# Second block's recurrent input projection by seven half products, in pairs of heads

## Chip, cores and metric

One NeuronCore of a Trainium2 chip runs the whole kernel. The metric is the device time of one execution in microseconds (us); less is better. The kernel before takes 2208.46 us (median of three runs, 2200.77 to 2210.29).

## What is computed

Two layers over 2048 tokens of width 1024, fp32. Layer 1 is a gated MLP with a spatial mix, layer 2 a gated linear recurrence. The change concerns the input projection of layer 2, `h @ w_in`, here for 12 heads of 128 columns, each with a recurrent column block (x) and a gate column block (g):

```python
xb, g = jnp.split(h @ w_in, 2, axis=-1)             # (2048 x 1024) @ (1024 x 3072)
xc = conv_b + conv_w[3] * xb + ...                  # causal convolution, 4 taps, per channel
r = sigmoid(xh @ gate_a_w + gate_a_b)               # per head, 128 x 128
i = sigmoid(xh @ gate_x_w + gate_x_b)
a = exp(-8 * r * softplus(-lam))
hseq = scan(a, sqrt(1 - a * a) * (i * xc))          # h = a * h + b along the tokens
y = hseq * silu(g);  x = x + y @ w_out
```

## The kernel before

**Blocks and stages.** The 2048 tokens are taken in two blocks of 1024 (`NB`, index `i`). A block goes through layer 1's values (`a_values`), layer 1's gates (`a_gates`), layer 1's output projection (`out_round`, four rounds), layer 2's input projection with its heads (`b_branch`), and layer 2's output projection (`b_out`, and `b_close` in the last block). Channels lie on the 128 partitions, tokens along the free axis. State that crosses from block 0 to block 1 is the convolution's `halo` and the scan's `state`.

**Three passes.** fp32 operands are split into a high and a low part of type fp32r (`split`, L90: a cast on ScalarE, a subtraction on VectorE), and a product is three matmuls (`mm3`, L378: high-high, high-low, low-high). A matmul is 128 x 128 by 128 x 512.

**Half products.** Layer 1 multiplies 2 x 2 blocks with seven products in place of eight (Strassen's method in Winograd's form). The matrix is halved twice: features by columns of the weight, and tokens into two halves of 512. `prep_item` (L187) makes the seven weight operands of an item from two loads of 512 KB with four additions of 128 x 512 and seven splits; `Sums` (L549) makes the seven operands of the activations, each a tile of pool `tops` (14 slots). A `Pair` (L575) is one item: steps `p1` to `p7` of 12 matmuls each (four feature blocks by three passes), which accumulate into a PSUM tile `J` of two halves and a PSUM tile `Y`, with copies on ScalarE and additions on VectorE between them that give two output tiles `oa` and `ob`. A step that adds on into a half of `J` has to wait for the copy that reads that half. `run_pairs` (L625) interleaves the steps of a pair with the last two of the pair before: 1, -4, 5, -3, 6, 2, 7 (minus: of the pair before).

**Layer 2's input projection** is done with all eight blocks. `b_branch` (L998) takes head after head: `proj` (L1004) is 48 matmuls for x (tile `px`) and 48 for g (`pg`); then `Head.conv`, `gates` (12 matmuls into `pr` and `pi`), `decay`, `silu` and `scan` on VectorE and ScalarE, one head behind. The activations `hb` are eight tiles of `tops`; the RMS factor `rbb` multiplies `px` and `pg` as they are read from PSUM (L936, L957). The weights `wb` come from HBM and are split in both blocks (`prep_two`, L238).

**Order.** A list `stream` (L288 to L339) holds every weight tile in the order of use; `take` (L373) makes tiles up to four ahead and loads raw data up to eight ahead. Entries without a key (items made ahead) are made where they stand in the list and written to HBM (`keep`, L221); `load_item` (L228) reads them back in block 1, or later in block 0. In block 0's `a_gates` the eight items of the output projection are made ahead in this way. All transfers are issued on SyncE's queue (SP). Tiles come from pools: `wops` 8 (weight operands), `raws` 4, `work` 12 (tag `wk`: 128 x 1028 fp32; the heads' tiles, `x` and layer 1's `u` and `g`), `pjp` 3 of two PSUM banks, `pbp` 2 of one bank. The tile framework fixes each engine's order ahead of the run from the program's order and the dependencies, and puts an instruction that is ready ahead of one that is not.

Of the kernel before, what the change touches and what calls it, by code (L numbers as in the profile page):

```python
# [57 lines left out]
VP = {0: (1, 2, 6, 5, 7, 3, 4), 2: (1, 5, 6, 3, 7, 2, 4)}  # L58

I_V = N_ITEMS  # L60


@with_exitstack
def trunk(ctx: ExitStack, tc: tile.TileContext, xT, WI, WV, WB, WO, WG, par, wsT, bs, outT):
# [201 lines left out]

        return [((i, "g", b), make, load)]

    def woven(items, more={}):

        out, prev = [], None
        for k, it in enumerate([*items, None]):
            o = {key[2]: (key, f, load) for key, f, load in it} if it else {}
            for p in (1, -4, 5, -3, 6, 2, 7):
# [10 lines left out]
        [(None, f, load) for _, f, load in prep_item(0, m, keep=True, use=False)]  # L285
        for m in range(I_AO, N_ITEMS)
    ]
    stream = []  # L288
    for i in range(NB):
        for k, (c, _) in enumerate(VG[i]):  # L290
            units = prep_v(i, k, c)
            stream += units
        if i > 0:
            for p in VP[0]:
                for u in range(4):
                    make = load_item(i, I_V + u)[MADE.index(p)][1]
                    stream.append(((i, "vs", 0, p, u), make, None))
        stream += prep_vs(i)
        more = {}
        if i == 0:  # L300
            for k in range(0, 16, 2):
                n = ahead.pop(0)
                more |= {(k, 6): n[:3], (k, 2): n[3:6], (k, 7): n[6:]}
        stream += woven([prep_item(i, m) for m in range(I_UG, I_AO)], more)
        for m in range(I_AO, N_ITEMS):
            stream += load_item(i, m)
        for n in range(NH):
            tile_x, tile_g = (
                prep_two([(i, "b", n, z, u) for u in range(2)], f"b{i}_{n}{z}", WB[n, z])
                for z in range(2)  # L310
            )
# [313 lines left out]
    def run_pairs(pairs, hooks):  # L625

        prev = None
        for k, q in enumerate([*pairs, None]):
            steps = []
            if q is not None:  # L630
                steps.append(q.p1)
            if prev is not None:
                steps.append(prev.p4)
            if q is not None:
                steps.append(q.p5)
            if prev is not None:
                steps.append(prev.p3)
            if q is not None:
                steps += [q.p6, q.p2, q.p7]
            for n, f in enumerate(steps):  # L640
                f()
                for g in hooks.get((k, n), ()):
                    g()
            prev = q


# [275 lines left out]
    class Head:  # L922
# [9 lines left out]
        def conv(self, px, rb):  # L932

            n = self.n
            xb = work.tile([P, 1028], F32, tag="wk", name=f"xb{self.id}")
            nc.vector.tensor_tensor(  # L936
                xb[:, 3 : 3 + TB].rearrange("p (a t) -> p a t", a=2), px, rb, ALU.mult
            )
# [59 lines left out]
    def b_branch(i, hb, rb, hooks):  # L998
# [22 lines left out]
        for n in range(NH):  # L1021
# [17 lines left out]
            if n > 0:  # L1039
                heads[n - 1].scan()  # L1040
            after(n, 1)
        return yd, heads[-1]

    def load_yb(i, r, yd):

# [198 lines left out]
    for i in range(NB):  # L1244
# [90 lines left out]
        def ready_b(g, a, th, i=i, x=x, xd=xd, nm=nm, hb=hb):  # L1335
# [11 lines left out]
                nm[th].add(t)  # L1347
            return f

        after = {  # L1350
            (g, p): [ready_b(g, a, th)]
            for g in range(2)
            for p, a, th in ((2, 0, 0), (7, 1, 1), (3, 0, 1), (4, 1, 0))
        }
        for r in range(4):
            tp = sy.o
            if r < 3:
# [22 lines left out]
        yd, tail = b_branch(i, hb, rb, {(0, 0): [finish_b]})  # L1380
        y[0] = load_yb(i, 0, yd)
        x = {}
        last = i == NB - 1
# [2 lines left out]
        def reload(*keys, i=i, x=x, xd=xd):  # L1386
            def f():
                for k in keys:
                    x[k] = wk(f"xr{i}_{k[0]}{k[1]}{k[2]}")
                    nc.sync.dma_start(x[k], xd[k])  # L1390
            return f
# [8 lines left out]
                store(i, th, x, r)  # L1400
            return f

        def end_tail(tail=tail):
            tail.gates()
            tail.decay()
            tail.scan()
# [4 lines left out]
        hooks = {0: [end_tail, reload(*xk[2:])], 1: [get_y(2)]}  # L1411
# [18 lines left out]
def pack(a_w_in, a_w_out, b_w_in, b_gate_a_w, b_gate_x_w, b_w_out):  # L1430
# [13 lines left out]

    u, g = quarters(win[:, :AW]), quarters(win[:, 2 * AW :])
    ug = np.stack([u, g], 1).reshape(16, 2, P, 2, 512)
    items = np.concatenate([ug, outs(wout)], 0)

    wb = b_w_in[0].reshape(2, 4, P, 2, NH, P).transpose(4, 3, 2, 0, 1, 5)

# [54 lines left out]
```

## Time and profile before

| | |
|---|---|
| median of three runs | 2208.46 us |
| the profiled execution | 2206.12 us |
| its span in the trace | 2204.4 us |
| TensorE (PE) busy | 2181.9 us, 99% |
| VectorE (DVE) busy | 1573.5 us, 71% |
| ScalarE (ACT) busy | 1165.7 us, 53% |
| transfers | 371.96 MB, 169 GB/s |

The profiled execution is 2.3 us under the median. A busy share of 99% is an average over stages that have different second engines; the windows by stage say more.

### The profile page before, as it was taken

The page shows a single profiled execution, that of the slowest core. Times are in us where ns is not written, and L with a number is a line of the kernel's source. Part 1 is how long each engine was busy: PE and PEld are TensorE (multiplying, and loading weights), DVE is VectorE, ACT ScalarE, POOL GpSimd, SP SyncE. Part 2 cuts the span into 40 slices and gives each one's busy share as a digit, 9 for nine tenths or more (in the row PEclk, how much of TensorE's full clock was granted, in tenths as well). Part 3 has the DMA queues.
Part 4 walks back from the last instruction along what each step waited for, and adds up shares of the span by engine and source line. Part 5 has one row for each costly group of instructions (what it writes and reads, how often), then busy time and mean ns, then how long its engine had stood idle before and what let it go on. Part 6 is the DMA issues. An engine that isn't in the chain of part 4 may idle for free.

```text
span 2204.4 us, 26352 instructions
## 1 busy us (share of the span) xinstructions
PE 2181.9 (99%) x10016; PEld 1813.8 (82%) x10016; DVE 1573.5 (71%) x2004; ACT 1165.7 (53%) x1598; POOL 63.5 (3%) x83
## 2 busy tenths in 40 slices
PE   9999999999999999999999999999999999999998
PEld 7887878888888888888888888888888888888887
DVE  7967777776878778675776665665678767767735
ACT  7535665663225777774343455455522456777611
POOL 0000000000000001010000000000000001101000
PEclk9999999999999999999999999999999999999998
DMA  6565665669764544236276532232597512222412
GB/s 224 168 211 200 230 218 182 222 233 329 289 226 158 179 178 166 91 105 248 76 246 203 176 130 94 98 112 90 176 336 252 196 62 85 95 89 75 179 43 77
DMA packets 141087, 371.96 MB, mean 169 GB/s; under 512 B 11296, under 2 KB 29856, under 8 KB 140960
## 3 DMA queue, kind: packets, MB, share of 16 engines
q1 hardware_dynamic: 140960, 370.27, 48.4%
q8 instruction: 79, 1.29, 0.2%
q14 instruction: 48, 0.39, 0.1%
HBM read 261.70 MB, written 108.53 MB: 168 GB/s over the span
## 4 chain that ended last, share of the span: by engine, by line
PE 90%; DMA 4%; DVE 3%; ACT 2%; issue 1%; SPq 0%; DVEq 0%; ACTq 0%
PE px L380 18%; PE J L380 17%; PE pg L380 12%; PE po L380 10%; PE X L380 8%; PE Y L380 5%; PE pz L380 4%; PE Z L380 4%; PE pv L380 4%; PE ps L869 2%; DMA vl<-vd 2%; PE pc L380 2%; DMA raw<-in_w 2%; PE pi L380 2%; PE pr L380 2%
## 5 line engine op out<-in xcount | busy, mean ns | idle before, releaser
L380 PE MATMUL J<-ha,w 128*128 128x512 f32 x1728 | 411.0, 391 | 6.3 <-ACT u_0a L604 2.3
L380 PEld LDWEIGHTS J<-ha,w 128*128 128x128 f32 x1728 | 323.2, 188 | 77.0 <-ACT u_0a L604 3.2
L380 PE MATMUL px<-hb,wb 128*128 128x512 f32 x1152 | 266.8, 390 | 0.0
L380 PE MATMUL pg<-hb,wb 128*128 128x512 f32 x1152 | 266.0, 390 | 0.0
L380 PEld LDWEIGHTS pg<-hb,wb 128*128 128x128 f32 x1152 | 216.2, 188 | 45.6
L380 PEld LDWEIGHTS px<-hb,wb 128*128 128x128 f32 x1152 | 215.9, 188 | 44.7
L380 PE MATMUL po<-yb,wo 128*128 128x512 f32 x960 | 219.4, 390 | 0.0
L380 PEld LDWEIGHTS po<-yb,wo 128*128 128x128 f32 x960 | 179.9, 188 | 37.2
L380 PE MATMUL X<-ya,w 128*128 128x512 f32 x768 | 183.3, 390 | 0.0
L380 PEld LDWEIGHTS X<-ya,w 128*128 128x128 f32 x768 | 143.7, 188 | 30.3 <-ACT ya L92 0.4
L93 DVE TENSOR_TENSOR w<-raw,w 128x512 fp32r<-128x512 f32 x160 | 108.6, 687 | 65.5 <-ACT w L92 65.3
L92 ACT CAST ya<-ya 128x1024 fp32r<-128x1024 f32 x56 | 57.5, 1051 | 159.8 <-DVE ya L569 100.3
L380 PE MATMUL J<-b,w 128*128 128x512 f32 x576 | 140.2, 391 | 0.0
L92 ACT CAST w<-raw 128x512 fp32r<-128x512 f32 x160 | 97.5, 619 | 74.8 <-issue 39.7
L380 PEld LDWEIGHTS J<-b,w 128*128 128x128 f32 x576 | 107.1, 188 | 21.6
L670 DVE TENSOR_TENSOR x<-x,X 128x1024 f32<-128x1024 f32 x64 | 77.9, 1218 | 31.8 <-PE X L380 31.8
L380 PE MATMUL Y<-b,w 128*128 128x512 f32 x384 | 93.4, 392 | 1.3 <-DVE sp L873 1.2
L947 DVE SCALAR_TENSOR_TENSOR xc<-xb,pp,xc 128x1024 f32<-128x1024 f32 x72 | 92.3, 1281 | 3.4 <-ACT xc L943 2.6
L380 PE MATMUL Z<-ya,w 128*128 128x512 f32 x384 | 92.6, 389 | 0.0
L380 PEld LDWEIGHTS Y<-b,w 128*128 128x128 f32 x384 | 71.0, 188 | 17.7 <-DVE sp L873 3.0
L92 ACT CAST wb<-rb 128x512 fp32r<-128x512 f32 x96 | 57.8, 615 | 52.2 <-PE px L380 22.1
L380 PEld LDWEIGHTS Z<-ya,w 128*128 128x128 f32 x384 | 72.1, 188 | 15.0
(416 smaller groups left out, 3558.5 us busy)
## 6 DMA issues: line engine op xcount, KB each, us to landing
w<-keep SPq DMA_DIRECT2D x140, 512.0 KB, 3.8
keep<-wc SPq DMA_DIRECT2D x84, 512.0 KB, 3.8
raw<-in_w SPq DMA_DIRECT2D x64, 512.0 KB, 4.2
rb<-in_wb SPq DMA_DIRECT2D x48, 512.0 KB, 3.6
vd<-v SPq DMA_DIRECT2D x32, 512.0 KB, 3.0
vl<-vd SPq DMA_DIRECT2D x32, 512.0 KB, 5.1
ya<-ya SPq DMA_DIRECT2D x16, 1024.0 KB, 6.7
yb<-sg SPq DMA_DIRECT2D x24, 512.0 KB, 2.9
```

The costliest lines, as they stand in the source:

```text
L92: nc.scalar.copy(dst[:, 0], src)
L93: nc.vector.tensor_tensor(dst[:, 1], src, dst[:, 0].bitcast(F32), ALU.subtract)
L380: nc.tensor.matmul(out, lhsT=s, rhs=m, start=first and n == 0, stop=last and n == 2, skip_group_check=True,)
L670: nc.vector.tensor_tensor(t, t, acc[z], ALU.add)
L869: nc.tensor.matmul(pS[:, n * P : (n + 1) * P], lhsT=v[j][th][:, n, cc * P : (cc + 1) * P], rhs=wcv[:, j, :], start=True, stop=True,)
L947: nc.vector.scalar_tensor_tensor(xf, xb[:, k : k + TB], col(C_CW + 4 * n + k), xf, ALU.mult, ALU.add)
```

## The change

Block 1's input projection of layer 2 goes through `Pair`, block 0's stays as it is. The 24 column blocks become 12 items (`bi`): an x item and a g item for each two heads.

- **Weights made ahead.** `early_b` makes the 12 items with `prep_item(keep=True)`: the first in block 0's `b_branch` (after head 9), the next two in block 0's `b_out`, nine in block 1's `a_gates`, spread over 16 pairs. Block 1 reads the 84 operands back (`load_item`) and no longer loads and splits its 24 `wb` tiles.
- **Activations.** In block 1's last `out_round` the step `ready_b` (scale and split into eight tiles `hb`) is replaced by `ready_q` (scaled copies in eight `wk` tiles, on ScalarE) and `make_q` (the seven operands of `Sums` for each of two channel groups, 14 tiles of `tops`), and the squares of the norm come in later calls (`norm_q`). `rbb` moves from `tops` to a `wk` tile.
- **Pairs.** `b_pairs` runs 12 pairs in the order 1, 5, -4, 6, 2, -3, 7. The RMS factor is applied to the finished sums (`scale`, `c21`). `conv` then works on the tile in place. The first gates of a round stand behind `p2` of the next x pair, the second behind `p1` of the next g pair.
- **Tail.** Two heads are left for `b_out` in place of one, and `y[2]` is read back one group later.

```diff
+STEPS = (1, -4, 5, -3, 6, 2, 7)
+STEPS_B = (1, 5, -4, 6, 2, -3, 7)
...
+    def early_b(m):
+        return [
+            (None, f, load) for _, f, load in prep_item(
+                0, I_BI + m, keep=True, use=False, src=lambda m, h: WI[m - 4, h]
+            )
+        ]
...
+        else:
+            for k in range(9):
+                n = early_b(3 + k)
+                k = (1, 3, 5, 6, 8, 10, 11, 13, 15)[k]
+                more |= {(k, 6): n[:3], (k, 2): n[3:6], (k, 7): n[6:]}
...
-        for n in range(NH):
+        if i > 0:
+            stream += woven(
+                [load_item(i, I_BI + m) for m in range(N_BI)],
+                {(2 * b + 2, 2): prep_g(i, b) for b in range(5)} | {(12, -3): prep_g(i, 5)},
+                STEPS_B,
+            )
+        for n in range(NH if i == 0 else 0):
...
+            if n == 9:
+                stream += early_b(0)
         for a, g in AG:
+            if i == 0 and g == 0:
+                stream += early_b(1 + a)
...
+    def b_pairs(i, tp, rb, norm):
...
+        def c21(dst, src):
+            nc.vector.tensor_tensor(dst, src, rb[:, 0], ALU.mult)
+
+        def scale(oa, ob):
+            nc.vector.tensor_tensor(oa, oa, rb, ALU.mult)
+            nc.vector.tensor_tensor(ob[:, 1], ob[:, 1], rb[:, 1], ALU.mult)
+
+        def end_x(b):
+            def f(oa, ob):
+                scale(oa, ob)
+                for h in range(2):
+                    heads[2 * b + h].conv(xb[b][h], None)
+            return f
+
+        def end_g(b):
+            def f(oa, ob):
+                scale(oa, ob)
+                for h, t in enumerate((oa, ob)):
+                    nc.scalar.activation(t, t, AF.Silu)
+                    heads[2 * b + h].sg = t
+            return f
+
+        def first_part(n):
+            def f():
+                heads[n].gates()
+                heads[n].decay()
+            return f
+
+        for b in range(6):
+            pairs.append(Pair(i, I_BI + 2 * b, tp, outs_x(b), c21, end_x(b)))
+            pairs.append(Pair(i, I_BI + 2 * b + 1, tp, outs_g(b), c21, end_g(b)))
+            if b < 5:
+                hooks[2 * b + 2, "p2"] = [first_part(2 * b)]
+                hooks[2 * b + 2, "p7"] = [heads[2 * b].scan]
+                hooks[2 * b + 3, "p1"] = [first_part(2 * b + 1), heads[2 * b + 1].scan]
+        hooks[0, "p2"] = [norm]
+        run_pairs(pairs, hooks, STEPS_B)
+        return yd, heads[-2:]
...
+            after = {
+                (0, 2): [ready_q(0, 0, 0)],
+                (0, 7): [ready_q(0, 1, 1), make_q(0, 1)],
+                (0, 3): [ready_q(0, 0, 1), make_q(0, 5)],
+                (0, 4): [ready_q(0, 1, 0)],
+                (1, 1): [make_q(0, 6), norm_q(0, *every)],
+                (1, 6): [make_q(0, 2)],
+                (1, 2): [make_q(0, 7), ready_q(1, 0, 0)],
+                (1, 7): [ready_q(1, 1, 1), make_q(1, 1)],
+                (1, 3): [ready_q(1, 0, 1), make_q(1, 5)],
+                (1, 4): [
+                    ready_q(1, 1, 0), make_q(1, 6), make_q(1, 2), make_q(0, 4), make_q(1, 7),
+                    make_q(1, 4), make_q(0, 3), make_q(1, 3), norm_q(1, *every),
+                ],
+            }
...
-        rb = tops.tile([P, 2, 2, T], F32, tag="top", name=f"rbb{i}")[:, 0]
+        if i == 0:
+            rb = tops.tile([P, 2, 2, T], F32, tag="top", name=f"rbb{i}")[:, 0]
+        else:
+            rb = wk(f"rbb{i}")
...
+            hooks = {
+                0: [end_tail(tail[0]), reload(*xk[2:4])],
+                1: [end_tail(tail[1]), reload(*xk[4:])], 2: [get_y(2)],
+            }
```

## Rows read from the trace of the kernel before

**Rows 1.** The page: busy time by engine, and the granted clock in 40 slices

```profile
PE 2181.9 (99%) x10016; PEld 1813.8 (82%) x10016; DVE 1573.5 (71%) x2004; ACT 1165.7 (53%) x1598; POOL 63.5 (3%) x83
...
PEclk9999999999999999999999999999999999999998
```

**Rows 2.** Windows by stage; the first line names the columns

```profile
core 0: us, PE busy (x) PEld busy (x) DVE busy (x) ACT busy (x) POOL busy (x), PEclk, DMA share, GB/s
187.10:519.30 332.20, 325.66 (x1551) 270.94 (x1549) 252.93 (x359) 199.71 (x331) 0.00 (x0) 1.00 0.63 217
1271.70:1597.10 325.40, 324.34 (x1553) 271.87 (x1552) 200.69 (x279) 173.83 (x281) 0.00 (x0) 1.00 0.34 113
...
1752.50:2051.00 298.50, 298.50 (x1329) 246.87 (x1328) 213.68 (x215) 206.83 (x230) 29.29 (x33) 1.00 0.26 88
1600.00:1752.50 152.50, 152.50 (x673) 125.92 (x673) 120.33 (x115) 39.40 (x51) 0.19 (x1) 1.00 0.75 267
1714.40:1752.50 38.10, 38.10 (x169) 31.45 (x168) 29.37 (x36) 15.14 (x26) 0.00 (x0) 1.00 0.60 200
972.90:1100.00 127.10, 127.10 (x578) 105.53 (x577) 83.19 (x110) 57.85 (x79) 1.67 (x2) 1.00 0.43 153
2051.00:2140.70 89.70, 89.70 (x397) 74.21 (x397) 41.04 (x41) 34.51 (x41) 1.67 (x2) 1.00 0.31 112
```

**Rows 3.** TensorE's timeline in block 1's projection: start, length, line, names, count

```profile
1928.22 11.04 PE L380 MATMUL px<-hb,wb 128*128 128x512 f32 x48
1939.10 0.40 PE L380 MATMUL pr<-xch,wg 128*128 128x512 f32 x1
```

**Rows 4.** TensorE's waits in block 0's gate stage: total us, times, longest

```profile
PE J L380 <- ACT u_0a L604: 1.8, 1, 1.8
...
PE J L380 <- DVE u_3b L614: 1.3, 1, 1.3
```

**Rows 5.** VectorE's groups, block 1's projection (L1344: whole span): count, busy us, mean ns

```profile
L947 DVE SCALAR_TENSOR_TENSOR xc<-xb,pp,xc 128x1024 f32<-128x1024 f32 x36 | 46.1, 1282 | 2.9 <-ACT xc L943 2.3
L93 DVE TENSOR_TENSOR wb<-rb,wb 128x512 fp32r<-128x512 f32 x38 | 26.0, 687 | 9.7 <-ACT wb L92 9.7
L993 DVE TENSOR_TENSOR_SCAN xc<-a,state,gi 128x1024 f32<-128x1024 f32 x10 | 23.5, 2346 | 0.0
L936 DVE TENSOR_TENSOR xb<-px,rbb 128x1024 f32<-128x1024 f32 x12 | 14.6, 1218 | 0.2 <-ACT rbb L517 0.2
...
L1344 DVE SCALAR_TENSOR_TENSOR hb<-x,pp,hb 128x512 fp32r<-128x512 f32 x32 | 22.9, 748 | 2.2 <-ACT hb L1343 2.1
```

**Rows 6.** ScalarE's groups in block 1's projection

```profile
L92 ACT CAST wb<-rb 128x512 fp32r<-128x512 f32 x38 | 23.2, 616 | 34.2 <-PE px L380 17.2 <-PE pg L380 17.0
L943 ACT ACTIVATE xc<-xb,pp 128x1024 f32<-128x1024 f32 x12 | 15.0, 1252 | 9.7 <-DVE xb L936 9.7
...
L974 ACT ACT_TABLE_LOAD x11 | 14.1, 1283 | 0.6 <-PE pr L380 0.4
L976 ACT ACTIVATE gi<-pi,pp 128x512 f32<-128x512 f32 x22 | 13.9, 686 | 0.0
...
L982 ACT ACTIVATE a<-r,c 128x1024 f32<-128x1024 f32 x10 | 11.5, 1154 | 0.1
```

**Rows 7.** ScalarE's timeline: a table load and the activation behind it

```profile
1952.79 1.28 ACT L982 ACT_TABLE_LOAD   x1
1954.09 1.15 ACT L982 ACTIVATE a<-r,c 128x1024 f32<-128x1024 f32 x1
```

**Rows 8.** Timelines: a loaded head's last product, and the tail head's chain

```profile
1966.66 1.23 DVE L995 TENSOR_TENSOR sg<-xc,sg 128x1024 f32<-128x1024 f32 x1
...
2072.80 0.40 PE L380 MATMUL pr<-xch,wg 128*128 128x512 f32 x1
...
2089.02 2.35 DVE L993 TENSOR_TENSOR_SCAN xc<-a,state,gi 128x1024 f32<-128x1024 f32 x1
...
2091.87 1.22 DVE L995 TENSOR_TENSOR sg<-xc,sg 128x1024 f32<-128x1024 f32 x1
```

More of the change, by code (lines that the diff above doesn't have):

```diff
@@ L60 @@
 I_V = N_ITEMS
+I_BI = N_ITEMS + 4
+N_BI = 12
+STEPS = (1, -4, 5, -3, 6, 2, 7)
+STEPS_B = (1, 5, -4, 6, 2, -3, 7)
 @with_exitstack
@@ L267, in prep_g, with woven @@
         return [((i, "g", b), make, load)]
-    def woven(items, more={}):
+    def woven(items, more={}, order=STEPS):
         out, prev = [], None
@@ L273, in woven @@
             o = {key[2]: (key, f, load) for key, f, load in it} if it else {}
-            for p in (1, -4, 5, -3, 6, 2, 7):
+            for p in order:
                 if p > 0 and it:
@@ L623, in p3, with run_pairs @@
             self.finish(self.oa, self.ob)
-    def run_pairs(pairs, hooks):
+    def run_pairs(pairs, hooks, order=STEPS):
         prev = None
         for k, q in enumerate([*pairs, None]):
[L629 to L642, printed above, removed]
+            n = 0
+            for p in order:
+                which = q if p > 0 else prev
+                if which is None:
+                    continue
+                getattr(which, f"p{abs(p)}")()
+                for g in [*hooks.get((k, n), ()), *hooks.get((k, f"p{p}"), ())]:
                     g()
+                n += 1
             prev = q
@@ L934, in conv @@
             n = self.n
[L935 to L938, printed above, removed]
+            if rb is None:
+                xb = px
+            else:
+                xb = work.tile([P, 1028], F32, tag="wk", name=f"xb{self.id}")
+                nc.vector.tensor_tensor(
+                    xb[:, 3 : 3 + TB].rearrange("p (a t) -> p a t", a=2), px, rb, ALU.mult
+                )
             nc.gpsimd.tensor_copy(xb[:, 0:3], halo[:, n, :])
@@ L1041, in b_branch, with outs_x, outs_g, f @@
             after(n, 1)
-        return yd, heads[-1]
+        return yd, heads[-1:]
+    def b_pairs(i, tp, rb, norm):
+        yd = [y_tile(f"yb{i}_{r}") for r in range(3)]
+        gw, xb, hooks, pairs = {}, {}, {}, []
+        heads = [Head(i, n, gw, yd) for n in range(NH)]
+        def outs_x(b):
+            def f():
+                xb[b] = [
+                    work.tile([P, 1028], F32, tag="wk", name=f"xb{i}_{b}{h}") for h in range(2)
+                ]
+                return tuple(
+                    t[:, 3 : 3 + TB].rearrange("p (a t) -> p a t", a=2) for t in xb[b]
+                )
+            return f
+        def outs_g(b):
+            return lambda: (wk(f"sga{i}_{b}"), wk(f"sgb{i}_{b}"))
+        def c21(dst, src):
[17 more added lines that the diff above has]
+        def first_part(n):
+            def f():
+                heads[n].gates()
+                heads[n].decay()
+            return f
+        for b in range(6):
[8 more added lines that the diff above has]
+        return yd, heads[-2:]
     def load_yb(i, r, yd):
@@ L1348, in ready_b, with ready_q, f, make_q @@
             return f
[L1350 to L1354, printed above, removed]
+        if i == 0:
+            after = {
+                (g, p): [ready_b(g, a, th)]
+                for g in range(2)
+                for p, a, th in ((2, 0, 0), (7, 1, 1), (3, 0, 1), (4, 1, 0))
+            }
+        else:
+            q = {0: {}, 1: {}}
+            sb = {g: Sums(f"hb{i}_{g}", q[g]) for g in range(2)}
+            def ready_q(g, a, th, x=x, xd=xd, q=q):
+                def f():
+                    t = x[a, th, g]
+                    nc.sync.dma_start(xd[a, th, g], t)
+                    q[g][a, th] = wk(f"hq{i}_{a}{th}{g}")
+                    for kk in range(2):
+                        nc.scalar.activation(
+                            q[g][a, th][:, kk], t[:, kk], AF.Copy,
+                            scale=col(C_NB + 4 * g + 2 * kk + a),
+                        )
+                return f
+            def make_q(g, *ps, sb=sb):
+                return lambda: sb[g].make(*ps)
+            def norm_q(g, *keys, nm=nm, x=x):
+                def f():
+                    for a, th in keys:
+                        nm[th].add(x[a, th, g])
+                return f
+            every = ((0, 0), (0, 1), (1, 1), (1, 0))
+            after = {
+                (0, 2): [ready_q(0, 0, 0)],
[12 more added lines that the diff above has]
+            }
         for r in range(4):
@@ L1365, in trunk @@
                 sy.make(*USED)
-        rb = tops.tile([P, 2, 2, T], F32, tag="top", name=f"rbb{i}")[:, 0]
+        if i == 0:
+            rb = tops.tile([P, 2, 2, T], F32, tag="top", name=f"rbb{i}")[:, 0]
+        else:
+            rb = wk(f"rbb{i}")
         def finish_b():
@@ L1378, in get_y @@
             return f
-        yd, tail = b_branch(i, hb, rb, {(0, 0): [finish_b]})
+        if i == 0:
+            yd, tail = b_branch(i, hb, rb, {(0, 0): [finish_b]})
+        else:
+            yd, tail = b_pairs(i, [sb[0].o, sb[1].o], rb, finish_b)
         y[0] = load_yb(i, 0, yd)
@@ L1401, in end_f, with end_tail, f @@
             return f
[L1403 to L1406, printed above, removed]
+        def end_tail(h):
+            def f():
+                h.gates()
+                h.decay()
+                h.scan()
+            return f
         y[1] = load_yb(i, 1, yd)
@@ L1410, in trunk @@
         reload(*xk[:2])()
-        hooks = {0: [end_tail, reload(*xk[2:])], 1: [get_y(2)]}
+        if i == 0:
+            hooks = {0: [end_tail(tail[0]), reload(*xk[2:])], 1: [get_y(2)]}
+        else:
+            hooks = {
+                0: [end_tail(tail[0]), reload(*xk[2:4])],
+                1: [end_tail(tail[1]), reload(*xk[4:])], 2: [get_y(2)],
+            }
         if not last:
@@ L1446, in pack @@
     ug = np.stack([u, g], 1).reshape(16, 2, P, 2, 512)
-    items = np.concatenate([ug, outs(wout)], 0)
+    bx, bg = quarters(b_w_in[0][:, :BW]), quarters(b_w_in[0][:, BW:])
+    bi = np.stack([bx, bg], 1).reshape(12, 2, P, 2, 512)
+    items = np.concatenate([ug, outs(wout), bi], 0)
     wb = b_w_in[0].reshape(2, 4, P, 2, NH, P).transpose(4, 3, 2, 0, 1, 5)
```

## The prediction

> **What bounds the kernel now.** I read the busy times first, then the windows by stage, then TensorE's timeline. [...] The windows show that no other engine is full in any stage: in block 1's projection stage (1752.5 to 2051.0 us) TensorE is busy all 298.5 us, VectorE 213.7 us (72%), ScalarE 206.8 us (69%), and the transfers take 26% [rows 2]. A run of 48 matmuls lasts there from 1928.22 to 1939.10, so one costs 10.88 / 48 = 226.7 ns [rows 3]. That price holds as long as the next operand is there in time.
>
> **What is removed.** Block 1's projection has 24 column blocks of 48 matmuls, 1152; after the change 12 pairs of seven steps of 12, 1008. The gates stay at 12 matmuls a head. 144 x 226.7 ns = **-32.6 us**, all on TensorE and so on the path. This is arithmetic on the program, so I give no chance to the change not doing what it says. Two heads take 2 x 108 matmuls = 49.0 us before and 192 = 43.5 us after. The 48 casts and 48 subtractions of block 1's `wb` tiles go too [rows 5, 6]; they are hidden today, and leaving them away only makes room.
>
> **Weights made ahead: +7 us.** An item is four additions and seven subtractions of 128 x 512 on VectorE (11 x 0.687 = 7.6 us, [rows 5]) and seven casts on ScalarE (7 x 0.616 = 4.3 us, [rows 6]), two loads and seven stores.
> - Nine items go into block 1's gate stage. Block 0's gate stage is the same work with eight such items in it, so it is the nearest row: it lasts 332.2 us against 325.4 in block 1, with 6.5 against 1.1 us of TensorE idle [rows 2]. Its waits are for ScalarE's copies and VectorE's additions out of `J` [rows 4]: those stand behind the extra splits in queues that are served in order. For nine items that is (332.2 - 325.4) x 9/8 = 7.6 us by the lengths and 5.4 x 9/8 = 6.1 by the idle time; I take 7. The lower bound is 0 (other places in the stage, VectorE has 125 us free [rows 2]), the upper 10.
> - Three items go into the end of block 0's layer 2: 23 us of VectorE and 13 of ScalarE. Block 0's output projection alone has 44 us of VectorE and 69 of ScalarE free, and TensorE is busy throughout [rows 2]. Cost nothing; without that cover, at the gate stage's rate of 6.8 / 8 an item, 2.5 us.
> - Transfers: the 12 items add 12.6 MB of reads and 44 MB of writes, block 1 reads 44 MB back and saves 12.6. Block 0's gate stage bore 217 GB/s, and the output rounds live on 267 GB/s of operands read back, with TensorE busy 152.5 of 152.5 us [rows 2]. The projection stage comes to 88 + (44 - 12.6) MB / 266 us = some 206 GB/s. Cost nothing; a late operand would be the next thing to see.
>
> **The activations, at the seam: +3 us.** The last output round lasts 38.1 us [rows 2]. VectorE has 14 additions of 1.22 us in it. The two `Sums` add 2 x (7 + 4) operations of 128 x 1024, at 1.22 us 26.8 us [rows 5], in place of 16 scaled subtractions of 0.75 us, 12 us [rows 5]: +15 us, in a stretch where VectorE has 38.1 - 29.4 = 8.7 us free [rows 2]. So some 6 us run over into the first pair. What is late there: of channel group 1 the operands for `p5` and `p6` can only start when the last but one product is drained, and each is a chain of subtraction, cast, subtraction of some 3.5 us. TensorE has `p1` and the first halves of `p5` (4 us) to go on with. I take 3 us; bounds 0 and the whole 15.
>
> **The pairs: +5 us.** For two heads, VectorE: per pair four operations of 128 x 512 and a scaling of 1.22 + 0.69, 4.7 us, twice 9.3; six of the convolution at 1.282; two scans at 2.346; ten of 128 x 1024 at 1.22; one split [rows 5]: 34.7 us of 43.5, 80%. ScalarE: seven copies and casts of 128 x 512 at 0.616; two of 1.252; four of the gates' at 0.686; fourteen more of 128 x 1024 (cast, SiLU, sigmoid, exponential, tanh, square, root) at some 1.1, a little under the exponential's 1.154; eight table loads of 1.283 [rows 6]: 35 us, 80%. So both stay under TensorE, but their share rises by 8 to 11 points, and TensorE now waits on them in finer steps: a copy out of `J` has two products, 5.4 us, before the next step needs that half. Nothing before shows such pairs beside heads. Bound from below: 0, as the stage runs now [rows 2]. From above: the slot rival below, 35 us. The nearest row is block 0's gate stage, the same pairs at 76% of VectorE with 6.5 us idle in 332.2 [rows 2]: 2.0% of 6 x 43.5 us is 5 us.
>
> What else is moved has one answer. The reads of `y[0]` wait for `tops` tiles, which all 14 hold operands until the last pair: they come free step by step over its last 20 us, and TensorE needs the second of the two rounds only 10.9 us into `b_out`. The second tail head's gates come some 44 us into a stage of 89.7 us plus one gate group; the tail head's chain of 20.3 us [rows 8], write and read back, and four splits fit. Cost nothing.
>
> **Sum.** 2206.1 - 32.6 + 7 + 3 + 5 = 2188.5 us for the profiled execution, which lies 2.3 us under the median: **2191 us**.
>
> [...] A table load takes 1.28 us and the activation behind it starts at 1954.09, 0.02 us after its end [rows 7]; eight loads for two heads are 10.4 us. [...]
>
> **Rivals.**
> - **Copies caught behind a head's run on ScalarE: about 2206 us, no change.** A head's sigmoids, exponential, tanh and square with two table loads are 2.6 + 1.1 + 1.4 + 3 x 1.1 = 8.4 us in one run [rows 6]; a copy out of `J` that stands behind it has 5.4 us of cover, so 3.0 us are lost. One in each of five rounds is 15 us on top of the 5. For: ScalarE goes to 80%, and a wait of this form, 1.8 us, is the longest for `J` in block 0 [rows 4]. Against: the order is planned, and in the gate stages such waits are few. ScalarE as the bound, by the rule above, comes out at the same time; I give that 0.02 of this case's 0.25.
> - **Work slots: about 2221 us, slower.** Of the 12 `wk` slots `rbb` now holds one for the whole stage, and two heads want 16 tiles a round. When the second head's gates have run, its `r` and `gi` need slots that the first head (its `xc`, `r`, `gi`, `a`, with `sg`) still holds until its scan is through; until then `pi` keeps both one-bank PSUM tiles, and the next `p2` has no `Y`. From the first head's gates to that `p2` the steps take (12 + 36 + 12 + 36) matmuls x 226.7 ns = 21.8 us. The tail head, on its own, goes from gates to the end of its scan in 2091.37 - 2072.80 = 18.6 us, which with the sigmoid of 1.4 fits [rows 8]. A head in the loaded stage now takes 1967.89 - 1939.10 = 28.8 us to its last product [rows 3, 8], 7.0 us too long: five rounds, 35 us in place of 5, a time of 2221 us. It decides at about 20 us from gates to scan. For: both engines get busier than they are in the loaded case. Against: there the next head's convolution stands between gates and decay, and in the change it doesn't; waiting TensorE also lets the others catch up.
>
> **How the numbers follow.** A measurement of this kernel can tell about 0.5%, 11 us: faster is under 2197.4 us, slower over 2219.5. The forecast has 0.64, the copies 0.25, the slots 0.11. The forecast's own range is 2176 (no stall at all: 2206.1 + 2.3 - 32.6) to 2197. The range for all is **2177 to 2213 us**: from one microsecond over that bound it takes in the copies' case, with room for the seam's upper bound, and leaves out most of the slots' case. Faster 0.64, same 0.25, slower 0.11.
>
> **What would show it.** [...] The copies' case: waits of `J` for ScalarE's copies of 2 to 3 us once a round. The slots' case: `Y` or `pr` waiting for `gi` or a sigmoid, some 7 us a round. Wrong altogether: waits for operands read back, a granted clock at the lower level in the stage, or a stage of TensorE that is not shorter although its matmuls are fewer.

## The result, and the profile after

The changed kernel takes **2269.4 us** (median of four runs, 2269.1 to 2274.5), the kernel before 2206.9 in the runs beside it: a ratio of 1.0293 [1.0281, 1.0305], slower by some 62 us. The forecast was 2191 us, the range 2177 to 2213.

The profiled execution of after has a span of 2267.4 us, 63.0 more than before. Its page, busy time and granted clock, against [rows 1]:

```profile
PE 2187.8 (96%) x9872; PEld 1804.6 (80%) x9872; DVE 1661.6 (73%) x2142; ACT 1221.6 (54%) x1688; POOL 60.6 (3%) x83
...
PEclk9999999999999999999999999999999888999999
```

The 144 matmuls are gone (10016 to 9872), and yet TensorE is busy 6 us longer: in three slices its clock is lower. Windows by stage, with the columns of [rows 2]:

```profile
core 0: us, PE busy (x) PEld busy (x) DVE busy (x) ACT busy (x) POOL busy (x), PEclk, DMA share, GB/s
1770.19:2203.36 433.17, 385.22 (x1568) 308.62 (x1566) 263.10 (x267) 249.08 (x275) 28.34 (x36) 0.91 0.46 152
...
1614.70:1769.80 155.10, 152.07 (x667) 124.70 (x666) 125.08 (x111) 43.66 (x53) 0.33 (x1) 1.00 0.79 280
972.80:1110.00 137.20, 133.81 (x595) 109.70 (x594) 100.79 (x133) 68.00 (x95) 2.45 (x3) 0.99 0.55 200
1800.00:1850.00 50.00, 42.95 (x161) 34.20 (x160) 19.44 (x27) 16.95 (x23) 0.74 (x4) 0.78 0.31 99
```

The first line is block 1's projection with the output projection behind it, from the last product of layer 1 to the first `pc`: 433.2 us. Before, the same stretch took 384.1 us without a gap:

```profile
1756.76:2140.88 384.12, 384.12 (x1708) 317.68 (x1706) 250.46 (x250) 237.53 (x264) 30.96 (x35) 1.00 0.27 92
```

It should have become 384.1 - 32.6 = 351.5 us, so **81.7 us are lost here**: 433.2 - 385.2 = 48.0 us in which TensorE waits, and 385.2 - 351.5 = 33.7 us by which its matmuls are slower. The rest of the 63 us lies ahead: 5.7 us at block 0's end, 4.6 in block 1's gate stage, 3.1 in the output rounds (by the first products of each stage, after against before); TensorE had no gap at block 0's end and in the output rounds [rows 2], and now has 137.2 - 133.8 = 3.4 and 155.1 - 152.1 = 3.0 us. What ended the waits in the projection (total us, times, longest):

```profile
PE pr L408 <- ACT xch L977: 16.5, 5, 3.4
PE J L408 <- ACT xb L625: 14.2, 5, 3.2
PE po L408 <- DVE yb L99: 6.9, 2, 6.2
PE J L408 <- DMA w<-keep: 3.5, 1, 3.5
PE bc_b L544 <- DVE nd_b L543: 3.0, 1, 3.0
PE pr L408 <- DVE xcl L978: 1.6, 3, 0.5
PE J L408 <- ACT sga L625: 1.4, 1, 1.4
PE pi L408 <- ACT xch L977: 0.7, 1, 0.7
```

The first two come once a round (two heads, that is one x pair and one g pair), in five rounds. (L972 is the convolution of a head into its tile `xc`; L977 is the cast of `xc` to its high part `xch`, which the gates multiply; L625 is the copy in `p1`, L641 and L642 are copy and addition in `p7`.) One such place on TensorE, start and length first:

```profile
1877.90 2.88 PE L408 MATMUL Y<-hb,w 128*128 128x512 f32 x12
1884.16 0.80 PE L408 MATMUL pr<-xch,wg 128*128 128x512 f32 x1 [3.38 <-ACT xch L977]
...
1887.29 0.63 PE L408 MATMUL pr<-xch,wg 128*128 128x512 f32 x1
1887.72 0.63 PE L408 MATMUL pi<-xcl,wg 128*128 128x512 f32 x1
1888.14 0.63 PE L408 MATMUL pi<-xch,wg 128*128 128x512 f32 x1
1891.38 10.96 PE L408 MATMUL J<-hb,w 128*128 128x512 f32 x36 [2.61 <-ACT xb L625]
```

TensorE does `p1` and `p2` of the new x pair (to 1880.8), then wants the first head's gates, waits 3.4 us for the cast, and wants `p5`, and waits 2.6 us for the copy behind `p1`. After the waits matmuls start 0.43 us apart in place of 0.227: the granted clock is 0.50 from 1884 to 1890 us and from 1891.38 to 1896, where it was 1.00 from 1850 to 1878. The 36 matmuls at 1891.38 take 10.96 us, where 36 take 8.3 to 8.4 elsewhere in the round. Of the 33.7 us by which matmuls are slower, some 24 are of this kind (about 108 matmuls start late by some 0.2 us each); the rest is the ends of interrupted runs of matmuls and delays too short for the list of waits. From 1750 to 2150 us the granted clock is 0.78 to 0.94 in every 50 us.

ScalarE's and VectorE's timelines say why both are late:

```profile
1883.06 1.04 ACT L977 CAST xch<-xc 128x1024 fp32r<-128x1024 f32 x1 [6.17 <-DVE xc L972]
1884.01 1.24 ACT L968 ACTIVATE xc<-xb,pp 128x1024 f32<-128x1024 f32 x1
1889.31 1.04 ACT L977 CAST xch<-xc 128x1024 fp32r<-128x1024 f32 x1 [4.06 <-DVE xc L972]
1890.26 0.58 ACT L641 COPY sgb<-J 128x512 f32<-128x512 f32 x1
1890.74 0.59 ACT L625 COPY xb<-J 128x512 f32<-128x512 f32 x1
```

```profile
1875.53 2.34 DVE L1018 TENSOR_TENSOR_SCAN xc<-a,state,gi 128x1024 f32<-128x1024 f32 x1
1877.91 1.22 DVE L1020 TENSOR_TENSOR sgb<-xc,sgb 128x1024 f32<-128x1024 f32 x1
1879.05 3.92 DVE L972 SCALAR_TENSOR_TENSOR xc<-xb,pp,xc 128x1024 f32<-128x1024 f32 x3
...
1885.35 3.92 DVE L972 SCALAR_TENSOR_TENSOR xc<-xb,pp,xc 128x1024 f32<-128x1024 f32 x3
...
1891.53 0.68 DVE L642 TENSOR_TENSOR sgb<-sgb,J 128x512 f32<-128x512 f32 x1
```

`p1` ends at 1878.06; its copy starts at 1890.74. In front of it in ScalarE's queue stand the casts of both heads, each of which waits for three operations of the convolution on VectorE. ScalarE stands idle for 6.2 and 4.1 us before them. Over the five rounds:

```profile
L977 ACT CAST xch<-xc 128x1024 fp32r<-128x1024 f32 x10 | 10.4, 1044 | 49.0 <-DVE xc L972 49.0
```
Ten casts of 1.04 us, and 49.0 us of idle time in front of them. The copy, ready for 12.7 us, did not pass the casts.

My theory after this: not the engines' work but **the order of their queues** costs the time, and a wait is paid in part a second time in the clock. Rivals: the engines are too slow for a round; the work slots; the steps' order.

### The profile page after: what moved, and what is told of

The parts are those of the page before. It is cut to its first block, busy times and chain, and to the rows that moved or that the text cites. A ratio compares the mean times of both kernels' runs of the same rounds, so it can differ in the third digit from the quotient of the medians.

```text
span 2267.4 us, 26755 instructions
## 1 busy us (share of the span) xinstructions
PE 2187.8 (96%) x9872; PEld 1804.6 (80%) x9872; DVE 1661.6 (73%) x2142; ACT 1221.6 (54%) x1688; POOL 60.6 (3%) x83
## 4 chain that ended last, share of the span: by engine, by line
PE 78%; DVE 9%; DMA 5%; ACT 5%; issue 3%; SPq 0%; DVEq 0%; ACTq 0%
PE J L408 24%; PE px L408 10%; PE po L408 9%; PE X L408 7%; PE Y L408 6%; PE pz L408 4%; PE pg L408 4%; PE pv L408 4%; PE Z L408 4%; DMA raw<-in_w 2%; DVE xc L972 2%; PE ps L891 2%; DMA vl<-vd 2%; PE pc L408 1%; PE pi L408 1%
## 5 line engine op out<-in xcount | busy, mean ns | idle before, releaser
L408 PE MATMUL J<-hb,w 128*128 128x512 f32 x864 | 217.2, 411 | 19.2 <-ACT xb L625 14.2
L408 PE MATMUL po<-yb,wo 128*128 128x512 f32 x960 | 225.7, 395 | 10.3 <-DVE yb L99 7.3
L408 PEld LDWEIGHTS J<-hb,w 128*128 128x128 f32 x864 | 171.7, 200 | 61.4 <-ACT xb L625 17.8
L408 PE MATMUL px<-hb,wb 128*128 128x512 f32 x576 | 133.5, 390 | 0.0
L408 PE MATMUL pg<-hb,wb 128*128 128x512 f32 x576 | 133.0, 390 | 0.0
L408 PEld LDWEIGHTS pg<-hb,wb 128*128 128x128 f32 x576 | 108.1, 188 | 22.9
L408 PEld LDWEIGHTS px<-hb,wb 128*128 128x128 f32 x576 | 107.9, 188 | 22.3
L692 DVE TENSOR_TENSOR x<-x,X 128x1024 f32<-128x1024 f32 x64 | 77.9, 1217 | 33.8 <-PE X L408 33.7
L99 DVE TENSOR_TENSOR wc<-rawc,wc 128x512 fp32r<-128x512 f32 x120 | 80.4, 685 | 19.0 <-ACT wc L98 18.1
L972 DVE SCALAR_TENSOR_TENSOR xc<-xb,pp,xc 128x1024 f32<-128x1024 f32 x72 | 92.2, 1280 | 2.2 <-ACT xc L968 1.4
```

The source lines that it names most:

```text
L99: nc.vector.tensor_tensor(dst[:, 1], src, dst[:, 0].bitcast(F32), ALU.subtract)
L408: nc.tensor.matmul(out, lhsT=s, rhs=m, start=first and n == 0, stop=last and n == 2, skip_group_check=True,)
L692: nc.vector.tensor_tensor(t, t, acc[z], ALU.add)
L972: nc.vector.scalar_tensor_tensor(xf, xb[:, k : k + TB], col(C_CW + 4 * n + k), xf, ALU.mult, ALU.add)
```

## The experiments

### Which half of the change costs what (e3, e4)

Run e3 is the kernel before with the 12 items made ahead and not used. Run e4 is the change without making them; it reads back other saved operands in their place, so it leaves that part of the computation out.

```diff
-                nc.sync.dma_start(t.bitcast(F32), saved[m, p])
+                src = saved[m, p] if m < I_BI else saved[I_AO + (m - I_BI) % 8, p]
+                nc.sync.dma_start(t.bitcast(F32), src)
```

> The kernel before, which also makes the twelve items ahead and writes them to HBM, but doesn't read or use them; block 1 projects as before. By the stage lengths of the changed kernel (6 us more at block 0's end, 4 in block 1's gate stage, 0 to 3 in the output rounds): 2217 to 2222 us. Rival C (the weights made ahead are the main cost): over 2240 us. By the prediction's terms: 2214 us.

> The changed kernel without the making ahead of the twelve items: the pairs read back the operands of layer 1's output projection in their place (as many bytes; the projection's result is another one). Theory A: only the 10 to 13 us of the making go, 2255 to 2260 us. Rival C: under 2235 us.

Measured: e3 2221.4 us, 1.0072 [1.0053, 1.0091]; e4 2254.1 us, 1.0220 [1.0203, 1.0238]. The items cost some 16 us, and the pairs cost some 48 where they should give 32.6; together that is 64.6 us, against the change's 62.5. (e4 came out 1 us under its range.) Three of e3's waits, block 0's end and block 1's output rounds:

```profile
PE po L399 <- ACT wo L95: 2.6, 1, 2.6
PE X L399 <- issue: 1.6, 1, 1.6
PE X L399 <- DVE x L689: 1.0, 1, 1.0
```

### Is it work or waiting (e1, e2, e8)

Run e1 does the cast of `xch` on VectorE. Run e2 issues the 12 matmuls of `p2` twice in five x pairs, 60 x 226.7 ns = 13.6 us more for TensorE, ahead of its wait of up to 3.4 us for the first head's cast. Run e8 holds one more work slot through the stage.

```diff
-            nc.scalar.copy(self.ch, xc)
+            (nc.vector.tensor_copy if rb is None else nc.scalar.copy)(self.ch, xc)
...
             self.mm(2, y, True)
+            if self.twice:
+                self.mm(2, y, True, self.w2)
...
+        held = wk("held")
+        nc.gpsimd.memset(held[:, 0, 0:1], 0.0)
         run_pairs(pairs, hooks, STEPS_B)
+        nc.gpsimd.tensor_copy(halo[:, 0, 0:1], held[:, 0, 0:1])
```

> The changed kernel, with the cast to the high part of the convolved tile done on VectorE in block 1's pairs; the order of everything else is the same. Theory A (the copies out of J stand in ScalarE's queue behind the two heads' casts, which wait for VectorE's convolution): ScalarE's idle time before the casts, 49 us in the stage, goes, the waits of J for the copy of xb fall from 14.2 us to under 4, and the time falls by 15 to 40 us, to 2230 to 2255 us. Rival B (both engines are simply too full, or work slots are short): VectorE has 10 instructions more, the gaps stay, 2265 to 2285 us.

> [...] If the fall of the granted clock after each gap is half of the price (theory A with the clock), the gap is filled, the gates and the next steps run at the upper level, and the time is no longer than before or falls by up to 15 us: 2255 to 2270 us. If only the idle time counts, 3.4 of the 2.7 us are hidden each time at best and the time stays within 3 us; if TensorE's time is the bound, 2280 to 2285 us.

> Edit: the changed kernel with one more of the 12 work slots held through the whole stage. Rival of the prediction (work slots set the round): the second head's tiles wait for a slot longer, 10 to 35 us more, 2280 to 2305 us. Theory (queues behind the convolution): slots are not what ends the waits, 2264 to 2275 us, no difference.

Measured: e1 2246.1 us, 1.0188 [1.0167, 1.0208]; e2 2268.6 us, 1.0285 [1.0264, 1.0306]; e8 2270.8 us, 1.0304 [1.0283, 1.0324]. The first waits of e1, then of e2:

```profile
PE pr L408 <- DVE xch L977: 15.3, 5, 3.1
PE po L408 <- DVE yb L99: 7.6, 3, 6.2
```

```profile
PE J L408 <- ACT xb L630: 20.4, 5, 4.1
...
PE pr L408 <- ACT xch L984: 2.9, 5, 0.7
```

In e2 13.6 us of matmuls cost nothing: the wait for the cast shrank by 13.6 us, and the next one grew by 6.2. TensorE is not what sets the round. In e1 the wait of `p5` for the copy is gone, and 23 us with it, though the wait was only 14.2 us: the rest is in the matmuls (376.8 us busy in the stretch, 385.2 in after), with a granted clock of 0.986 over the run against 0.978. One slot less changes nothing, so the slots are out.

### The order of the queues (e5, e6, e7, e17, e9, e12)

Run e5 moves only the second head's convolution (`late` returns that call), to behind `p5` of the next x pair. Run e6 adds e1's cast; e7 adds to e6 layer 1's step order; e17 is that step order alone.

```diff
                 scale(oa, ob)
-                for h in range(2):
-                    heads[2 * b + h].conv(xb[b][h], None)
+                heads[2 * b].conv(xb[b][0], None)
...
+        for b in range(6):
+            hooks.setdefault((2 * b + 2, "p5" if b < 5 else "p-4"), []).append(late(b))
...
-        run_pairs(pairs, hooks, STEPS_B)
+        run_pairs(pairs, hooks, STEPS)
```

> Edit: only the second head's convolution of each x pair moves, to behind p5 of the next x pair; casts stay on ScalarE. Theory (copies out of J queue up behind work that waits for the convolution, and TensorE's clock falls after each gap): the copies of p7 and p1 now stand behind one head's cast and no longer behind two, some 5 us sooner; the wait of p5 for the copy (14.2 us in five) goes, the wait of the first gates for the first head's cast (16.5 us) stays. Time 2240 to 2256 us, 13 to 29 less than the change, about what moving the cast to VectorE gave. Rival (VectorE as a whole is too slow, order is no matter): 2263 to 2272, no gain. Rival (the gate products' wait alone sets the round): 2260 to 2270.

> Edit: as the run before, and the cast of both heads on VectorE. Theory: no copy out of J stands behind any cast, and the additions that free J stand behind one convolution only; left are the first gates' wait for the first head's cast (some 3 us a round, 15 in all) and what the clock loses behind it. Time 2236 to 2246 us. Rival (the gates' wait alone sets the round once the copies are free): the same as with the cast on VectorE and the old order, 2243 to 2249.

> Edit: as the run before, and the steps in layer 1's order 1, -4, 5, -3, 6, 2, 7. Theory: p5 has another product between it and p1, so its copy has 2.7 us of cover, but the first gates are still planned right behind p1 and p2, so their wait of some 3 us a round stays: 2232 to 2248 us. Rival (the order of the steps is what costs): under 2225 us.

> Edit: the changed kernel with nothing changed but the order of the steps, 1, -4, 5, -3, 6, 2, 7 as in layer 1, so that p5 no longer stands right behind p1. Theory (the copies are late because they stand behind the casts, however much cover they have): the wait of p5 for the copy only moves to p4 of the pair before, which needs the copy and addition of p7 from the same queues; 2258 to 2272 us. Rival (the missing cover between p1 and p5 is what costs): the wait of 14.2 us and the lower clock behind it go, 2240 to 2252 us.

Measured: e5 2245.9 us, 1.0191 [1.0175, 1.0206]; e6 2239.1, 1.0166 [1.0149, 1.0183]; e7 2234.6, 1.0141 [1.0123, 1.0158]; e17 2254.8, 1.0224 [1.0207, 1.0241]. Moving one convolution by a few places, with not one operation fewer, gave as much as e1. In e17 the wait of J for the copy of `p1` stayed:

```profile
PE J L408 <- ACT xb L625: 16.4, 5, 3.6
```

```profile
1883.61 12.81 PE L408 MATMUL J<-hb,w 128*128 128x512 f32 x48 [3.14 <-ACT xb L625]
```

But e17 does not test the cover that `p4` was to give. These 48 matmuls start 0.05 us after the copy has ended (1883.56), while `p7`'s addition, on whose semaphore `p4`'s first matmul waits in the trace, ends only at 1884.44: in the planned order the first matmuls of `p5` stand ahead of `p4` all the same. So no run separates the missing cover from the queue at this place. That the place in the queue is enough is shown by e5, where this wait is gone with the steps in their old order. What e17 gained, 15 us, came from the gates' waits (18.8 to 10.2 us) and from the matmuls (385.2 to 376.1 us busy in the stretch); its time lies between the theory's range and the rival's.

All of these keep the first gates' wait, because their first products are planned right behind `p2`, ahead of `p5`. Run e9 (on e6) ties them to the copy of `p6`: one column of `xch` is written again after it. Run e12 (on e9) writes the convolutions of both heads behind what frees J: the first behind `p7`'s addition, the second behind `p6`.

```diff
+    def hold(head, late):
+        ch, xc = head.ch, head.xc
+        nc.vector.scalar_tensor_tensor(
+            ch[:, 0, 0:1], late, 0.0, xc[:, 0, 0:1], ALU.mult, ALU.add
+        )
...
+                if n % 2 == 0:
+                    hold(heads[n], xb[n // 2 + 1][0][:, 3 + T : 4 + T])
                 heads[n].gates()
...
+            hooks.setdefault((2 * b + 1, "p7"), []).insert(0, late(2 * b))
+            hooks.setdefault((2 * b + 2, "p6" if b < 5 else "p-4"), []).insert(0, late(2 * b + 1))
```

> Edit: as the run with the second convolution later and the cast on VectorE, and the first gates of a round are tied to the copy behind p6 of the next x pair by one more tiny instruction on VectorE (it writes one column of the head's high part again), so that they cannot be planned right behind p2. Theory: the wait of the first gates for the cast (15.3 us in five) goes and with it the lower clock behind it; a round takes 43.5 to 45 us. 2216 to 2228 us. Rival (VectorE or ScalarE is too slow for a round of 43.5 us): the wait turns up elsewhere, J for a copy or an addition, and the time stays at 2233 to 2241.

> Edit: as the run with the first gates tied to p6 (cast on VectorE), and the convolutions of both heads are written behind the copy and addition of the g pair's p7 (first head) and behind p6 of the next x pair (second head), so that no addition or copy that frees a half of J stands behind a convolution. Theory (order in the two queues is what costs, not how much work they have): the waits of J for the additions L642 and L1095 (18.9 us) and for the copy (4.2) go, and nothing else takes their place; a round takes 43.5 to 45.5 us, 2218 to 2232 us. Rival (VectorE or ScalarE cannot do a round in less than some 50 us, in whatever order): the waits only move once more, 2237 to 2255.

Measured: e9 2252.6 us, 1.0217 [1.0190, 1.0244], a miss; e12 2234.2, 1.0139 [1.0123, 1.0155], 2 us over what was expected. The waits of e9:

```profile
PE J L408 <- DVE sgb L642: 11.6, 5, 2.5
PE po L408 <- ACT yb L98: 7.3, 2, 4.9
PE J L408 <- DVE sgb L1095: 7.3, 4, 1.8
PE J L408 <- ACT sga L625: 4.2, 6, 1.4
```

With the gates out of the way TensorE came sooner to steps that need a half of J, and those halves are freed by additions (L642, L1095, the latter `c21`) that stand behind the convolutions in VectorE's queue. The wait moved, and was dearer than the one removed (13.5 us over e6). The rival had said that it would move, but its time, 2233 to 2241, was passed too. And slow engines are not why it became dearer: in e12, where the additions stand ahead of the convolutions, the two waits fell to 10.6 us, of which 7.1 at the tail, and 18 us were won with no operation fewer.

### The ends and the items (e10, e11, e13, e15, e14, e16)

Run e10 is the change with the three items of block 0's end made in block 1's values (spread over 24 of its last 28 weight tiles). Run e11 joins e9, e10 and the norm's products one step later. Run e13 joins e12 and e10, issues both reads of `y[0]` ahead of their splits, and puts head 11's convolution behind `b_out`'s first group. Run e15 makes six items in the values, six in the gate stage, in the kernel before and unused (beside e3). Run e14 is e13 with those six, head 10's convolution also in `b_out`, and the norm behind the second pair's `p1`; e16 is e14 with three items in the values.

```diff
-                stream += early_b(0)
...
-                stream += early_b(1 + a)
...
+        vs = prep_vs(i)
+        if i > 0:
+            for k in range(3):
+                e = early_b(k)
+                for q in range(4):
+                    stream += vs[8 * k + 2 * q : 8 * k + 2 * q + 2] + e[2 * q : 2 * q + 2]
...
-                0: [end_tail(tail[0]), reload(*xk[2:4])],
+                0: [tail[0].late, tail[1].late, end_tail(tail[0]), reload(*xk[2:4])],
```

> Edit: the changed kernel, but the three items that are made ahead at block 0's end (first of them behind head 9, two in the output projection) are made in block 1's values. Theory: their 6 us at block 0's end go, and the values stage, where both engines are idle for half of the time, takes them for nothing: 2261 to 2266 us. Rival (every item costs its 0.8 us or more wherever it is made): 2267 to 2272.

> Edit: the kernel with the gates tied to p6, the three items in the values, and the norm's products one step later. Theory: sum of the parts, 2208 to 2222 us; against the kernel before it is the same or a little slower, because the seam, the tail and the nine items in the gate stage still cost what they did.

> Edit: the run before, and with it the three items in block 1's values, both reads of y[0] issued ahead of their four splits, and the last head's convolution behind b_out's first group. Theory: another 8 for the items and some 5 for the tail: 2204 to 2220 us, about the time of the kernel before, since seam, tail and the nine items still cost some 20 us. Rival (rounds bound by the two engines): 2225 to 2245.

> Edit: the kernel before with the 12 items made ahead and not used, as in the run on the weights alone, but six of them in block 1's values, six in its gate stage and none at block 0's end. Theory: the 6 us at block 0's end and a third of the gate stage's go: 2208 to 2215 us against 2221 for the first place. Rival (an item costs the same wherever it is made): 2218 to 2224.

> Edit: as the run with the best order and ends, and three more changes of place: the last two heads' convolutions both behind b_out's first group, the norm's products behind the second pair's p1, and six items (not three) in block 1's values with six left in the gate stage. Theory: the tail's waits for VectorE (7 us) and the norm's (3) go, the gate stage loses a third of its cost (3): 2207 to 2216 us, still a little over the kernel before. Rival (each of these places is bound by the engines and not by order): 2218 to 2226.

> Edit: the kernel with both last convolutions in b_out and the norm's products behind the second pair's p1, but three items in block 1's values as in the run with the best order and ends, nine in the gate stage. Theory: the 34 us that six items cost in the values (there TensorE waited for casts of ws, at 0.92 to 0.94 of the transfers' share) do not arise with three; the ends of the projection stage are some 10 us better than in the run with the best order and ends (2223): 2209 to 2217 us. Rival (part of the 34 us was the ends' new order): 2220 or more.

Measured: e10 2261.9 us, 1.0258 [1.0235, 1.0280]; e11 2238.4, 1.0159 [1.0142, 1.0175]; e13 2222.8, 1.0094 [1.0077, 1.0110]; e15 2257.7, 1.0242 [1.0228, 1.0256]; e14 2256.7, 1.0244 [1.0225, 1.0264]; e16 **2212.6**, 1.0038 [1.0024, 1.0051].

e10 shows that the three items need not cost what they did at block 0's end (7 us less). e11 inherits e9's miss, and e13 came out 3 us over its range. e15 and e14 missed by far: six items in the values cost 36 us more than e3's places. Two windows of e15 in the values, and its first waits there:

```profile
1200.00:1250.00 50.00, 40.59 (x148) 28.03 (x146) 33.45 (x53) 22.84 (x37) 0.00 (x0) 0.93 0.81 300
1250.00:1300.00 50.00, 33.69 (x111) 21.98 (x109) 36.74 (x59) 19.67 (x29) 0.00 (x0) 0.88 0.94 359
```

```profile
PE px L406 <- ACT ws L95: 12.8, 10, 4.8
PE pz L406 <- ACT ws L95: 11.1, 9, 2.6
```

VectorE and ScalarE have room, and the stage's own weights (`ws`) are late. The share of the transfers (0.94, 359 GB/s) looks like the cause, but it does not decide by itself. Three items left TensorE without a gap at 0.90 in e10, and at 0.93 (320 GB/s) in the same 50 us of e16, while e15 has 9.4 us of gaps at 0.81:

```profile
1200.00:1250.00 50.00, 50.00 (x222) 41.41 (x221) 39.55 (x61) 26.81 (x42) 0.00 (x0) 1.00 0.90 311
```

In e15 (1150 to 1320 us) the casts of `ws` wait 29.0 us for TensorE and 3.1 us for writes of items. What they wait for there is a free tile of `wops`, of which there are eight, and an item's operand holds one until its write has landed (some 6.8 us). Whether the tiles or the transfers are short, no run separates: this cause stays open.

e16 then shows the ends mended. A round of two heads in after, one in e16, e16's stretch from layer 1's last product to `pc`, and its first waits in the projection:

```profile
1884.16:1939.21 55.05, 49.03 (x192) 38.74 (x192) 33.75 (x32) 35.03 (x37) 5.09 (x6) 0.89 0.50 161
1919.94:1967.59 47.65, 44.87 (x192) 35.73 (x193) 34.35 (x34) 31.34 (x33) 4.36 (x6) 1.00 0.54 187
1764.33:2143.70 379.37, 361.32 (x1567) 291.89 (x1566) 267.44 (x284) 230.40 (x259) 24.98 (x36) 0.99 0.50 173
```

```profile
PE pr L415 <- DVE xch L1078: 3.5, 4, 0.9
PE J L415 <- DMA w<-keep: 3.3, 1, 3.3
PE J L415 <- ACT xb L639: 2.7, 4, 0.7
PE J L415 <- DVE sgb L1102: 2.6, 3, 0.9
```

The round went from 55.05 us to 47.65, with nearly the same work on VectorE (33.75 and 34.35 us) and 3.7 us less on ScalarE, which has given up the casts. The stretch is 379.4 us, 53.8 less than in after and 4.7 less than before. Of the 32.6 us that the pairs save, 27.9 are still lost here: 18.0 in waits, 9.8 in slower matmuls. The clock is the smaller part of these 9.8: it is 1.00 in the round shown and 0.99 over the stretch, and only 17 matmuls start 0.43 us apart, some 3.6 us. Outside the stretch e16 loses 9.5 us: 1.4 in block 0 (1.3 of it ahead of the output projection, where nothing was changed), none in the values, 3.4 in the gate stage, 2.8 in the output rounds, 1.9 at the end. So no version of the change beat the kernel before; the best is 0.38% slower.

**Open.** A round takes 47.1 to 49.2 us in e6, e12, e13 and e16, mostly 47.6, though the waits in it differ; before, it took 49.2. The 43.5 were not reached, and whether they can be is not settled: an engine that cannot do a round in less than 47 us is not ruled out. `p5` writes the other half of J than the copy reads, and still waits for it (in after, at 1891.38); separate tiles for the halves were not tried.

## Why the prediction was wrong

**"What is removed", -32.6 us: right.** 144 matmuls fewer, and they were worth their 226.7 ns as long as nothing was late. But a saving on TensorE counts only where TensorE sets the end, and here it stopped doing so.

**"The pairs: +5 us": the step that failed.** In the rounds TensorE waited 33.0 us for gates' operands and copies (16.5 + 14.2 + 1.6 + 0.7), and most of the 33.7 us of slower matmuls came with these waits; the seam's 7.9 and the tail's 6.9 us, below, are the other waits of the stretch. The work was sized well: for two heads I had 34.7 us on VectorE and 35 on ScalarE; the round from 1884.16 took 33.75 and 35.03. What failed are two inferences from these shares.
- "Both stay under TensorE", so only small stalls remain: I took a share of 80% as room. It is room only if what is wanted next is served next. The nearest row, block 0's gate stage at 76% with 2% idle [rows 2], has no heads in its queues; a head is a chain of scale, convolution, cast and subtraction on the two engines in turn.
- "A copy out of J has two products, 5.4 us, before the next step needs that half": `p5` follows `p1`, writes the other half and waits for that copy all the same, and the copy came 12.7 us late, not 3.

My rival "Copies caught behind a head's run on ScalarE" had the right wait (J for a copy, once a round, 2 to 3 us) and the wrong work in front of it: not sigmoids and exponentials, which would have run on, but casts that stood still for VectorE. It counted one wait a round; there were two, for the gates too. ScalarE as the bound, to which I gave 0.02, goes by a price of a table load that no run shows: in after a load takes 1.283 us, ScalarE is idle for 0.1 us in all before the ten sigmoids behind the loads of L999, and it had 49.0 us to spare before the casts alone. **Work slots** fell with e8.

**The clock.** My sums go by 226.7 ns a matmul throughout, and I had listed a lower granted clock under "Wrong altogether". It was 0.91 over the stretch, against 1.00 before, and the matmuls that start 0.43 us apart cost some 24 us, half a microsecond for each one of the 48.0 us of waiting. None of the sums had that factor, the rivals' neither: at this rate the copies' case, 15 us of waits, would have been 22 or 23, an estimate.

**"Weights made ahead: +7 us": 16 (e3).** The gate stage took 4.6 us in after, 6.3 in e3's profiled run and 3.3 to 3.4 in e10 and e16, less than the 7 each time; its waits in after are of `Y` for VectorE (3.4 of 4.5 us), not of `J` as in block 0 [rows 4]. The three items at block 0's end, "cost nothing; without that cover 2.5 us", took 5.7: in the output projection the longest wait of TensorE (2.6 us) is for casts of `wo` that stand behind an item's cast, and ScalarE waits 5.5 us for VectorE before that one (at 999.29): the same queueing on a smaller scale. The output rounds, which I had left out, took 3.1.

**"The activations, at the seam: +3 us": 7.9** (w<-keep 3.5, the norm 3.0, a copy 1.4), and TensorE's slowest 50 us behind it (0.78). The first of the three is a wait for an operand read back, which I had put at nothing under "Transfers" and listed under "Wrong altogether"; what made that operand late was not tested.

**The tail, "cost nothing": 6.9 us.** `po` was wanted at once, and its split stood behind the last scan and convolution on VectorE. In e16 no wait of `po` is left, by order and with the casts on VectorE.

## What to carry over

Before a change puts more chains that cross engines beside a TensorE that has no gaps, write down each engine's queue for one round and look for an operation that frees TensorE's next step and stands behind one that waits for another engine; busy shares do not show it. Count waits of some 3 us that come every round one and a half times or more: in after 48.0 us of waits came with 33.7 us of slower matmuls, some 24 of them in matmuls 0.43 us apart. Waits under 1 us mostly left the clock up here (0.99 over e16's stretch). And when work is moved to where the engines are idle, read also which tiles and which transfers that stage lives on.

## What the runs showed that I had not expected

- Waits of 3 us, once or twice in 50 us, were enough to bring matmuls to 0.43 us apart; in after's stretch 48.0 us of waits came with some 24 us of this. In e16 the rounds have waits of 0.3 to 0.9 us close to one another: from 1870.74 eight matmuls start 0.43 us apart behind them, while at 1919.94, behind the same waits one round later, none does (the granted clock is 1.00 there).
- 13.6 us of extra matmuls in e2 cost nothing (2268.6 against 2269.4 us).
- A wait can come back dearer: e9 took away e6's 15.3 us of waits for the cast, got 18.9 us of waits for additions, and took 13.5 us more in all.
- Six items in place of three took the values stage from no gap to 16 us of gaps in 50, at nearly the same share of the transfers (0.94 in e15, 0.93 in e16).
